# A transformer step on one core: the scale vector of the second norm made by VectorE in blocks of 256 features

## The chip, the core and the metric

The kernel runs on one core of a Trainium2 chip. The core has five engines with a queue of instructions each: TensorE (PE, matrix products; its weight loads are shown apart as PEld), VectorE (DVE), ScalarE (ACT), GpSimd (POOL) and SyncE (SP, which here only issues DMA transfers). An engine works its queue in order and waits for other engines and for transfers by semaphores. The metric is the device time of one execution in microseconds (us).

## What is computed

One layer of a hybrid backbone over 128 context and 512 latent tokens, with 2048 features, in float32. Each of the two halves of the layer is a norm with a scale and a shift, a mixer or a feed-forward net, and a norm with a gate:

```python
m = (jax.nn.silu(cv) @ w_ada + b_ada)[:, None, :]
sh1, sc1, g1, sh2, sc2, g2 = jnp.split(m, 6, axis=-1)     # one set for the context, one for the latents
h = rmsnorm(x, g_pre_mix) * (1 + sc1) + sh1
z = h @ w_in                                              # q, k, v of 8 heads; convolution; pooling
o = jnp.concatenate([a, cm, pm], axis=-1) @ w_out
x = x + g1 * rmsnorm(o, g_post_mix)
h = rmsnorm(x, g_pre_ffn) * (1 + sc2) + sh2
gt, up = jnp.split(h @ w_ffn_in, 2, axis=-1)
x = x + g2 * rmsnorm((jax.nn.silu(gt) * up) @ w_ffn_out, g_post_ffn)
```

The change is about `sc2`, the scale of the second norm: 2048 features for each of two conditionings, from a 2048 x 2048 slice of `w_ada` (16 MB).

## The kernel before

Features lie on the 128 partitions (16 tiles `kt`), tokens on the free axis, in two halves of 320. Each float32 product is made of three matmuls over high and low parts (`mm3`, L310 to L312): the weights of a *granule* (four tiles of 128 x 128) are split by ScalarE (L149, high) and VectorE (L150, low) into a tile `hl`. A list `items` is written in advance and worked off by `run_items`; before each item `prep_ahead` splits weights up to four granules ahead. Between granules `slot()` takes one step of each side task: convolution, pooling, `att_s` (scores, softmax, transposes to `pth`) and `att_v` (values, product `po`) of a head.

The order of the first part: pooling units and 24 units of q, k and v (`proj_unit`, four granules of 24 matmuls, loads of 512 KB on ScalarE's queue); then the output projection. Its first four feature blocks are worked in parts (`parts`, granules of 12 matmuls on the first half of the tokens), because the inputs come in late: `conv_final` (L493: a product on VectorE, then silu on ScalarE, then a split) makes the convolution's input and `put_cat` splits the stored outputs of heads and pooling. After two rounds of parts stands the pointwise product of the convolution (`wpw_use`, `cpw`), which needs the last split of `conv_final`. Then come plain granules for feature blocks 4 to 15 (first pass), and a second pass for the other half of the tokens, during which `chain` makes the second norm and first uses `sc2`.

The vectors of modulation 2, 3 and 4 (gate, shift, scale; `mods`) are made during the units: behind every second granule two items of 512 KB are loaded by SP into the ring `rb` of two buffers, and `mod1_use` (L204) multiplies each with the 32 columns of `s32` (two of them used) in four column tiles: four matmuls of 256 columns. After 32 items the sum lies in a bank, and `mod_finish` transposes it on VectorE and adds bias and gain. Vector 4, which is `sc2`, takes the last 32 items, in units 16 to 23 (heads 4 and 5, and q and k of head 6). Vector 5 is made later by VectorE (`mod5`, L1388 and L1390): blocks of 128 x 256, one instruction for each conditioning.

Of the kernel before, what the change touches and what calls it, by code (L numbers as in the profile page):

```python
# [16 lines left out]
P = 128  # L17
# [37 lines left out]
def trunk_kernel(ctx, tc, xT, small, wada0, wada1, wada2, win0, win, wout, wfi, wfo, ckT, cv, wpw, wpool, rpbT, invc,  # L55
# [283 lines left out]
    def proj_unit(src, evac, hooks):  # L339
        us = w_units(src)  # L340
        st = {}

        def use(g):
            def f(w):
                if g == 0:
                    st["ps"] = [bank("pj", "pj") for _ in range(2)]
                for hf in range(2):
                    for k in range(4):
                        kt = 4 * g + k
                        mm3(st["ps"][hf][:, :TH], w, k, act[hf][:, kt, 0, :], act[hf][:, kt, 1, :], kt == 0,  # L350
                            kt == KT - 1)
                if g == 3:
                    for hf in range(2):
                        evac(hf, st["ps"][hf])
                slot()
            return f
        for g in range(4):
            g_item(us[g // 2], g % 2, use(g))
            if g % 2:
                add_mods(2)  # L360
            if g in hooks:
                x_item(hooks[g])

    def x_item(f):
        items.append(("x", f))
# [5 lines left out]
    def opened(key, stack):  # L371
        P1[key] = stack.enter_context(tc.tile_pool(name=key, bufs=1, reuse_waits="tile"))
        return P1[key]
# [155 lines left out]
    def pool_side(g, up):  # L529
# [25 lines left out]
            act_e.activation(cat[:, s], ps[:, :TH], AF.Copy, scale=smv("pool_scale")[:, g:g + 1])  # L555
        act_e.dma_start(out=catd[g], in_=cat)

    def open_pool():
        accs.close()
        pm = opened("pm", pms)  # L560
        r = mxt([P, UP], "ps0", pool_=pm)[:, :4 * P].rearrange("p (g n) -> p g n", g=4)
        sp.dma_start(out=r, in_=wpool)
        t = cs["wpool"] = mxt([P, 2, 4, P], "wph", dt=F32R, pool_=pm)
        split(t[:, 0], t[:, 1], r)
# [198 lines left out]
        pool.dma_start(out=catd[4 + h if h < 4 else 8 + h], in_=cat)  # L763


    mods = [(v, kt, s) for v in (2, 3, 4) for kt in range(KT) for s in range(2)]

    def add_mods(n):

# [93 lines left out]
        P2["ss", 0] = p.tile([P, TH], F32, tag="ss", name="ss0")  # L863

    def begin_pass2():
        acts.close()
        q = XR.enter_context(tc.tile_pool(name="xr", bufs=1, side="right", reuse_waits="tile"))
        for i in (1, 2):
            t = q.tile([P, KP, 2, TH], F32R, tag=f"X{i}", name=f"X{i}")
            X[i] = [t[:, k] for k in range(KP)]  # L870
        add_slots(q, "r", KP)
        for k in range(KP):
            X["b", k] = slot_tile(f"ob{k}")
        P2["y2"] = yst.enter_context(tc.tile_pool(name="yp", bufs=1, side="right")).tile([P, TH], F32, tag="y2", name="y2")
        P3["e"] = eps.enter_context(tc.tile_pool(name="ep3", bufs=1, side="right", reuse_waits="tile"))
        p = P2["p", 1] = stb.enter_context(tc.tile_pool(name="ph2b", bufs=1, side="right", reuse_waits="tile"))
        P2["ss", 1] = p.tile([P, TH], F32, tag="ss", name="ss1")
        side.append(chain())
# [134 lines left out]
    def pass_unit(n, hf, parts=False):  # L1013
# [17 lines left out]
        us = w_units(wout[n])  # L1031
        for g in range(4):
            g_item(us[g // 2], g % 2, use(g))
            if hf and n == KT - 1 and g == 1:
                x_item(lambda: S3.fetch())

# [3 lines left out]
    for g in range(4):  # L1040
        if g == 2:
            us = w_units(wpw)
            for n in range(4):
                g_item(us[n // 2], n % 2, wpw_use(n))
        for i, p in enumerate(parts):
            p(g)
            if g < 2:
                x_item(lambda: next(fin, None))
            if g != 1:
                x_item(lambda: put_cat(1))  # L1050
# [947 lines left out]
```

## Time and profile before

| | |
|---|---|
| median of 3 runs | 2737.63 us (2736.96 to 2738.61) |
| the profiled execution | 2736.24 us, span of its trace 2734.5 us |
| TensorE busy | 2611.9 us (96%) |
| VectorE busy | 2027.8 us (74%) |
| ScalarE busy | 1192.6 us (44%) |
| column tiles of vectors 2 to 4 (L204) | 206.8 to 649.9 us, 768 records, 52.4 us busy |
| heads 4 to 7 | some 497 to 720 us |
| parts of the output projection | some 718 to 777 us |
| first plain pass | some 777 to 862 us |

Times in the trace are microseconds from the start of the span. A fp32 matmul has two records. "Idle before <- releaser" names what ended an engine's wait. A busy TensorE is not TensorE at its peak, since matmuls overlap; what a group of matmuls costs is read from the starts of the matmuls around it. The granted clock of TensorE is 1.00 for 2.4 GHz and 0.50 for 1.2 GHz.

### The profile page before, as it was taken

What the parts mean: (1) busy time and instruction counts of PE and PEld (TensorE: products, weight loads), DVE (VectorE), ACT (ScalarE), POOL (GpSimd) and SP (SyncE); (2) the same over time, 40 slices, a digit from 0 to 9 for tenths busy, and PEclk for the clock granted to TensorE, in tenths of its full rate; (3) what the DMA queues carried; (4) which work ended last, traced back from release to release, by engine and by line L of the source; (5) the groups of instructions that cost most, each with busy time, mean ns of one, the idle gap of its engine ahead of it and who ended that gap; (6) DMA issues with size and microseconds to landing.
All of it is one profiled execution on the core that took longest, in us unless ns stands there. A gap on an engine that the chain in (4) does not pass through costs nothing.

```text
span 2734.5 us, 48244 instructions
## 1 busy us (share of the span) xinstructions
PE 2611.9 (96%) x18874; PEld 2515.4 (92%) x18874; DVE 2027.8 (74%) x3248; ACT 1192.6 (44%) x2427; POOL 681.9 (25%) x572
## 2 busy tenths in 40 slices
PE   5999999999899988999999999999999899999996
PEld 4898998899899987999999999999999899999985
DVE  5558874443545779777888888888786899999966
ACT  4232333333554646333333333333333655555554
POOL 2300020000112435544333333333333111111112
PEclk9999999999999999999999999999999999999998
DMA  8856565653445774443333333333332433333343
GB/s 310 297 187 220 197 195 199 221 189 123 159 147 168 212 250 145 147 160 125 128 107 120 124 117 111 127 125 107 121 124 81 140 107 121 110 120 106 98 130 109
DMA packets 182708, 415.88 MB, mean 152 GB/s; under 512 B 17872, under 2 KB 99920, under 8 KB 181968
## 3 DMA queue, kind: packets, MB, share of 16 engines
q1 hardware_dynamic: 151568, 316.58, 35.2%
q10 hardware_dynamic: 27296, 82.33, 9.5%
q0 software_dynamic: 3616, 13.90, 1.4%
q8 instruction: 148, 2.42, 0.4%
q14 instruction: 80, 0.66, 0.1%
HBM read 373.01 MB, written 39.71 MB: 151 GB/s over the span
## 4 chain that ended last, share of the span: by engine, by line
PE 66%; DVE 17%; ACT 5%; issue 5%; DMA 3%; POOL 2%; ACTq 1%; SPq 0%; DVEq 0%; POOLq 0%
PE pj L310 7%; PE pj L311 7%; PE pj L312 7%; PE u L1167 7%; PE u L1165 7%; PE u L1166 7%; DVE hl L1122 5%; PE bb L1165 3%; PE bb L1167 3%; PE bb L1166 3%; ACT hl L1121 2%; DVE f L1390 2%; PE bc L1165 2%; PE bc L1167 2%; PE bc L1166 2%
## 5 line engine op out<-in xcount | busy, mean ns | idle before, releaser
L1167 PE MATMUL u<-X,hl 128*128 128x320 f32 x2464 | 767.6, 312 | 23.7 <-DVE hl L1122 23.4
L1165 PE MATMUL u<-X,hl 128*128 128x320 f32 x2464 | 767.6, 312 | 8.2 <-ACT hl L1121 4.5
L1166 PE MATMUL u<-X,hl 128*128 128x320 f32 x2464 | 762.8, 310 | 0.0
L310 PE MATMUL pj<-act,hl 128*128 128x320 f32 x1664 | 525.1, 316 | 8.8 <-ACT act L250 4.7
L311 PE MATMUL pj<-act,hl 128*128 128x320 f32 x1664 | 516.0, 310 | 1.2 <-DVE act L150 0.7
L312 PE MATMUL pj<-act,hl 128*128 128x320 f32 x1664 | 515.4, 310 | 0.0
L1167 PEld LDWEIGHTS u<-X,hl 128*128 128x128 f32 x2464 | 464.2, 188 | 34.7 <-DVE hl L1122 34.5
L1165 PEld LDWEIGHTS u<-X,hl 128*128 128x128 f32 x2464 | 464.2, 188 | 15.8 <-ACT hl L1121 8.1
L1166 PEld LDWEIGHTS u<-X,hl 128*128 128x128 f32 x2464 | 464.3, 188 | 0.3 <-issue 0.2
L310 PEld LDWEIGHTS pj<-act,hl 128*128 128x128 f32 x1664 | 314.1, 189 | 33.8 <-issue 15.7
L150 DVE TENSOR_TENSOR hl<-ra,hl 128x512 fp32r<-128x512 f32 x244 | 183.5, 766 | 191.8 <-ACT hl L149 191.3
L311 PEld LDWEIGHTS pj<-act,hl 128*128 128x128 f32 x1664 | 314.2, 189 | 3.5 <-DVE act L150 2.1
L312 PEld LDWEIGHTS pj<-act,hl 128*128 128x128 f32 x1664 | 314.2, 189 | 0.2 <-DVE hl L150 0.2
L1122 DVE TENSOR_TENSOR hl<-ra,hl 128x512 fp32r<-128x512 f32 x264 | 244.0, 933 | 43.0 <-ACT hl L1121 42.5
L1150 POOL TENSOR_TENSOR s<-ra 128x512 f32<-128x512 f32 x88 | 145.0, 1647 | 335.0 <-DMA ra<-in_wfi 116.9
L1121 ACT ACTIVATE hl<-ra 128x512 fp32r<-128x512 f32 x264 | 159.4, 625 | 132.0 <-PE u L1167 106.0
L1121 ACT ACTIVATE hl<-s 128x512 fp32r<-128x512 f32 x176 | 110.2, 626 | 236.7 <-DVE s L1147 197.3
L1122 DVE TENSOR_TENSOR hl<-s,hl 128x512 fp32r<-128x512 f32 x176 | 133.4, 762 | 82.0 <-ACT hl L1121 80.9
L149 ACT ACTIVATE hl<-ra 128x512 fp32r<-128x512 f32 x244 | 148.2, 631 | 100.8 <-PE pj L312 56.9
L1122 DVE TENSOR_TENSOR hl<-sy,hl 128x512 fp32r<-128x512 f32 x176 | 139.2, 791 | 67.6 <-ACT hl L1121 67.2
L1147 POOL TENSOR_TENSOR sy<-ra,sy 128x512 f32<-128x512 f32 x88 | 133.7, 1519 | 151.4 <-DVE hl L1122 151.4
L1150 POOL TENSOR_TENSOR T<-T,raw 128x384 f32<-128x384 f32 (+1 forms) x56 | 54.8, 979 | 457.2 <-DVE T L1150 438.0
(343 smaller groups left out, 4926.3 us busy)
## 6 DMA issues: line engine op xcount, KB each, us to landing
ra<-in_wfi SPq DMA_DIRECT2D x196, 512.0 KB, 4.2
rb<-in_wada SPq DMA_DIRECT2D x96, 512.0 KB, 5.5
ra<-in_wada SPq DMA_DIRECT2D x64, 512.0 KB, 6.2
ra<-in_win ACTq DMA_DIRECT2D x56, 512.0 KB, 4.8
ra<-in_wout ACTq DMA_DIRECT2D x56, 512.0 KB, 4.1
raw<-in_wfo SPq DMA_DIRECT2D x48, 576.0 KB, 4.0
f<-in_wada SPq DMA_DIRECT2D x128, 128.0 KB, 2.1
fd<-f ACTq DMA_DIRECT2D x44, 320.0 KB, 2.2
```

The lines of the kernel that those rows point to most:

```text
L149: act_e.activation(h, src, AF.Copy)
L150: dve.tensor_tensor(out=l, in0=src, in1=h.bitcast(F32), op=ALU.subtract)
L310: pe.matmul(ps, w[:, 0, k, :], rhs_h, start=start, stop=False)
L311: pe.matmul(ps, w[:, 0, k, :], rhs_l, start=False, stop=False)
L312: pe.matmul(ps, w[:, 1, k, :], rhs_h, start=False, stop=stop)
L1121: act_e.activation(g.hl[:, 0, :n], src, AF.Copy)
L1122: dve.tensor_tensor(out=g.hl[:, 1, :n], in0=src, in1=g.hl[:, 0, :n].bitcast(F32), op=ALU.subtract)
L1147: e.tensor_tensor(out=out, in0=a, in1=b, op=ALU.subtract)
L1150: e.tensor_tensor(out=out, in0=a, in1=b, op=ALU.add)
L1165: pe.matmul(ps, w[:, 0, j, :], xh, start=first and j == 0, stop=False, skip_group_check=True)
L1166: pe.matmul(ps, w[:, 0, j, :], xl, start=False, stop=False, skip_group_check=True)
L1167: pe.matmul(ps, w[:, 1, j, :], xh, start=False, stop=stop and j == n - 1, skip_group_check=True)
```

## The change

Vector 4 leaves `mods`. In units 16 to 27 one or two steps (`dm_step`) stand behind each granule (1, 2, 1, 2), behind each part and behind each plain granule of the first pass one. A step takes one block of 128 x 256 weights from a ring of two buffers `dw` and runs two VectorE instructions, one for each conditioning: the first time for a column range it writes `macc`, later it multiplies with a scalar of `s32` and adds. Then SP loads the block after next into the buffer that this step has read. The two accumulators take the place of the ring `rb`. After 64 steps (half of the features), `dm_finish` sums over the partitions by eight matmuls with 32 columns of ones, and VectorE transposes and adds bias and gain. 128 steps make the vector: 72 in units 16 to 27, 16 in the parts, 40 in the plain pass.

```diff
             g_item(us[g // 2], g % 2, use(g))
-            if g % 2:
+            if not mods:
+                dm_item(1 + g % 2)
+            elif g % 2:
                 add_mods(2)
...
+    def dm_fetch(n):
+        for s, kt, j in DMS[dm["f"]:dm["f"] + n]:
+            t = dm["p"].tile([P, 256], F32, tag="dw", bufs=2, name="dw")
+            sp.dma_start(out=t, in_=wada1[2, kt, s][:, 256 * j:256 * j + 256])
+            dm["raw"].append(t)
+            dm["f"] += 1
+
+    def dm_step(n):
+        for s, kt, j in DMS[dm["c"]:dm["c"] + n]:
+            if kt == 0 and j == 0:
+                dm["acc"] = [wpb.tile([P, 1024], F32, tag="rb", bufs=2, name="macc") for _ in range(2)]
+                if s == 0:
+                    dm_fetch(2)
+            raw = dm["raw"].pop(0)
+            for c in range(2):
+                a, w = dm["acc"][c][:, 256 * j:256 * j + 256], s32[:, kt, c:c + 1]
+                if kt == 0:
+                    dve.tensor_scalar(out=a, in0=raw, scalar1=w, scalar2=None, op0=ALU.mult)
+                else:
+                    dve.scalar_tensor_tensor(out=a, in0=raw, scalar=w, in1=a, op0=ALU.mult, op1=ALU.add)
+            dm["c"] += 1
+            dm_fetch(1)
+            if kt == KT - 1 and j == 3:
+                dm_finish(s)
+
+    def dm_finish(s):
+        ps = bank("md", "mod4")
+        for c in range(2):
+            for j in range(4):
+                pe.matmul(ps[32 * j:32 * j + 32, 256 * c:256 * c + 256], ones[:, :32], dm["acc"][c][:, 256 * j:256 * j + 256],
+                          start=c == 0, stop=c == 1, tile_position=(0, 32 * j), skip_group_check=True)
...
+    def dm_item(n):
+        if n:
+            x_item(lambda: dm_step(n))
...
-    mods = [(v, kt, s) for v in (2, 3, 4) for kt in range(KT) for s in range(2)]
+    mods = [(v, kt, s) for v in (2, 3) for kt in range(KT) for s in range(2)]
...
             g_item(us[g // 2], g % 2, use(g))
+            if not hf:
+                dm_item(1)
...
         for i, p in enumerate(parts):
             p(g)
+            dm_item(1)
```

TensorE's queue in a unit of heads 4 to 6, before: `mod` is the bank of the vector, `rb` the weights, `s_90` the conditioning, `pj` the bank of the unit, `act_80` and `act_81` the two halves of the tokens.

```order
L310 MATMUL pj<-act_81,hl 128x320
L311 MATMUL pj<-act_81,hl 128x320
L312 MATMUL pj<-act_81,hl 128x320
L204 MATMUL mod_4_5520<-rb,s_90 32x256 x8
L310 MATMUL pj<-act_80,hl 128x320
L311 MATMUL pj<-act_80,hl 128x320
```

Sixteen such groups of eight go; on TensorE there are now two, at the ends of the two halves, here in head 7:

```order
L310 MATMUL pj<-act_81,hl 128x320
L311 MATMUL pj<-act_81,hl 128x320
L312 MATMUL pj<-act_81,hl 128x320
L594 MATMUL mod_7546<-macc,ones 32x256 x8
L310 MATMUL pj<-act_80,hl 128x320
L311 MATMUL pj<-act_80,hl 128x320
```

The groups of 32 columns that stood behind every second granule now stand twice in all, and read `macc` in place of loaded weights.

VectorE's queue in the parts of the output projection, before (`hl<-ra` is the split of a granule's weights, `cac` holds the convolution's reciprocal deviation, `qhl` and `khl` two of its four inputs):

```order
L150 TENSOR_TENSOR hl<-ra,hl 128x512
L493 TENSOR_TENSOR qhl<-qhl,cac 128x640
L150 TENSOR_TENSOR hl<-ra,hl 128x512
L150 TENSOR_TENSOR act_80<-qhl,act_80 128x320
L150 TENSOR_TENSOR act_81<-qhl,act_81 128x320
L150 TENSOR_TENSOR hl<-ra,hl 128x512
L493 TENSOR_TENSOR khl<-khl,cac 128x640
```

The same place after the change:

```order
L150 TENSOR_TENSOR hl<-ra,hl 128x512
L584 SCALAR_TENSOR_TENSOR macc<-dw,s_90,macc 128x256 x2
L495 TENSOR_TENSOR qhl<-qhl,cac 128x640
L150 TENSOR_TENSOR hl<-ra,hl 128x512
L584 SCALAR_TENSOR_TENSOR macc<-dw,s_90,macc 128x256 x2
L150 TENSOR_TENSOR act_80<-qhl,act_80 128x320
L150 TENSOR_TENSOR act_81<-qhl,act_81 128x320
L150 TENSOR_TENSOR hl<-ra,hl 128x512
L584 SCALAR_TENSOR_TENSOR macc<-dw,s_90,macc 128x256 x2
L495 TENSOR_TENSOR khl<-khl,cac 128x640
```

A step of two instructions now stands behind each split of weights, ahead of the product of `conv_final` (now L495) and of the `act` splits.

SP's queue from head 7 to the output projection, after the change (before, the four loads from `cvd` followed the load of `cvt` directly, and no loads of `dw` stood behind them):

```order
L669 DMA out_nkT<-kC 128x128
L568 DMA dw<-in_wada 128x256 x6
L651 DMA out_nvT<-vF 128x128
L785 DMA cvt<-in_cv 128x128
L568 DMA dw<-in_wada 128x256 x2
L492 DMA chp<-cvd 128x640
L492 DMA qhl<-cvd 128x640
L492 DMA khl<-cvd 128x640 x2
L568 DMA dw<-in_wada 128x256 x54
```

The loads for `conv_final` moved behind two loads of blocks, each of which waits for a step on VectorE.

## Rows read from the trace of the kernel before

**Rows 1.** Busy time by stage: the stretch, its length, then busy us (instructions) of TensorE, its weight loads, VectorE, ScalarE and GpSimd, the granted clock of TensorE, the DMA share and GB/s. The stretches are the end of head 6, head 7 with the seam, the parts, and the first plain pass.

```profile
655.00:700.00 45.00, 45.00 (x309) 44.57 (x308) 16.70 (x40) 16.38 (x57) 4.61 (x8) 1.00 0.18 54
700.00:730.00 30.00, 24.17 (x156) 22.23 (x154) 20.70 (x53) 19.94 (x57) 5.91 (x11) 0.95 0.71 234
730.00:770.00 40.00, 38.18 (x243) 36.77 (x241) 21.73 (x43) 24.29 (x56) 1.08 (x2) 0.95 0.43 127
800.00:860.00 60.00, 60.00 (x411) 60.00 (x410) 25.39 (x35) 27.69 (x60) 7.94 (x9) 1.00 0.51 151
```

**Rows 2.** Instructions of TensorE in order of time from 720 to 772 us, those ahead of which it stood idle (in brackets: us and what ended it).

```profile
720.24 0.33 PE L712 MATMUL ptr<-ident,pt 128*128 128x128 f32 x1 [0.22 <-DVE pt L651]
...
729.69 0.69 PE L712 MATMUL ptr<-ident,pt 128*128 128x128 f32 x2 [4.86 <-DVE pth L715]
...
748.04 0.41 PE L310 MATMUL cpw<-act,hl 128*128 128x320 f32 x1 [1.43 <-ACT act L149]
...
771.13 0.42 PE L310 MATMUL pj<-act,hl 128*128 128x320 f32 x1 [0.49 <-ACT act L149]
```

**Rows 3.** TensorE around one group of column tiles in order of time, a weight load of another group that waited for its transfer, and the group of all such matmuls from 503 to 652 us (count, busy us, mean ns).

```profile
533.75 0.31 PE L312 MATMUL pj<-act,hl 128*128 128x320 f32 x1
533.99 1.07 PE L204 MATMUL mod<-rb,s 128*32 128x256 f32 x16
534.99 0.41 PE L310 MATMUL pj<-act,hl 128*128 128x320 f32 x1
535.25 0.31 PE L311 MATMUL pj<-act,hl 128*128 128x320 f32 x1
535.39 0.31 PE L312 MATMUL pj<-act,hl 128*128 128x320 f32 x1
...
526.19 0.16 PEld L204 LDWEIGHTS mod<-rb,s 128*32 128x32 f32 x8 [0.98 <-DMA rb<-in_wada]
...
L204 PE MATMUL mod<-rb,s 128*32 128x256 f32 x256 | 17.5, 386 | 0.5 <-DMA rb<-in_wada 0.5
```

**Rows 4.** The instructions by which VectorE makes vector 5 (ns least, median, most; first and last start), two of them and the next one in order of time, SP's load of the block after next behind them and the loads of 512 KB that follow it, and the time to landing of all such loads of 128 KB.

```profile
L1390 DVE SCALAR_TENSOR_TENSOR f<-f,vec,f x240: 469/476/1529, 1292.0 to 2049.0; 128x256 f32<-128x256 f32 x120
...
L1388 DVE TENSOR_SCALAR f<-f,vec x16: 340/344/1453, 1284.9 to 1966.0; 128x256 f32<-128x256 f32 x16
...
1307.49 0.87 DVE L1390 SCALAR_TENSOR_TENSOR f<-f,vec,f 128x256 f32<-128x256 f32 x2
1308.29 0.68 DVE L1122 TENSOR_TENSOR hl<-ra,hl 128x512 fp32r<-128x512 f32 x1
...
1308.39 0.33 SPq L1376 DMA_DIRECT2D f<-in_wada  x1
1308.83 0.85 SPq L1093 DMA_DIRECT2D ra<-in_wfi  x2
...
DMA to landing us min/median/max: 1.9/2.1/5.0
```

**Rows 5.** Head 6, in order of time: VectorE's last split before the scores and its first instruction on them, the last division of the softmax, and TensorE's transposes that need it.

```profile
652.19 0.68 DVE L150 TENSOR_TENSOR hl<-ra,hl 128x512 fp32r<-128x512 f32 x1
654.29 0.29 DVE L645 TENSOR_REDUCE rs<-scc 128x1 f32<-128x128 f32 x1 [0.27 <-PE scc L677]
667.55 0.42 DVE L651 TENSOR_SCALAR pt<-pt,rs 128x384 f32<-128x384 f32 x1
...
670.62 0.82 PE L712 MATMUL ptr<-ident,pt 128*128 128x128 f32 x6
```

**Rows 6.** VectorE in head 7 in order of time: the instructions ahead of which it stood idle for something other than ScalarE's half of a split of weights.

```profile
704.08 0.29 DVE L645 TENSOR_REDUCE rs<-scc 128x1 f32<-128x128 f32 x1 [0.20 <-PE scc L677]
...
704.71 0.56 DVE L641 CUSTOM_DVE_ANT_0 pt<-sc,mb 128x384 f32<-128x384 f32 x1 [0.15 <-PE sc L684]
...
708.93 0.69 DVE L641 CUSTOM_DVE_ANT_0 pt<-sc,mb 128x512 f32<-128x512 f32 x1 [0.55 <-PE sc L684]
...
715.23 0.56 DVE L641 CUSTOM_DVE_ANT_0 pt<-sc,mb 128x384 f32<-128x384 f32 x1 [0.32 <-issue]
...
724.98 0.29 DVE L150 TENSOR_TENSOR vhl<-cvt,vhl 128x128 fp32r<-128x128 f32 x1 [0.54 <-ACT vhl L149]
```

**Rows 7.** VectorE in the parts, in order of time, over one loop of two parts.

```profile
736.65 0.82 DVE L493 TENSOR_TENSOR qhl<-qhl,cac 128x640 f32<-128x640 f32 x1
738.97 0.69 DVE L150 TENSOR_TENSOR hl<-ra,hl 128x512 fp32r<-128x512 f32 x1 [1.51 <-ACT hl L149]
739.58 0.89 DVE L150 TENSOR_TENSOR act<-qhl,act 128x320 fp32r<-128x320 f32 x2
740.39 0.68 DVE L150 TENSOR_TENSOR hl<-ra,hl 128x512 fp32r<-128x512 f32 x1
740.99 0.82 DVE L493 TENSOR_TENSOR khl<-khl,cac 128x640 f32<-128x640 f32 x1
```

**Rows 8.** The stretch behind TensorE's gap of 4.86 us (columns as in rows 1), and the fifteen `po` matmuls on the chain that ended last (start, us), in head 6 and in head 7.

```profile
731.00:733.00 2.00, 2.00 (x9) 1.81 (x8) 1.80 (x5) 1.27 (x4) 0.00 (x0) 0.50 0.63 167
...
683.56 2.45 PE po L753 x15
...
730.63 3.88 PE po L753 x15
```

**Rows 9.** VectorE in the last parts, in order of time.

```profile
767.10 0.69 DVE L150 TENSOR_TENSOR hl<-ra,hl 128x512 fp32r<-128x512 f32 x1 [0.33 <-ACT hl L149]
767.71 0.89 DVE L150 TENSOR_TENSOR act<-kF,act 128x320 fp32r<-128x320 f32 x2
768.93 0.69 DVE L150 TENSOR_TENSOR hl<-ra,hl 128x512 fp32r<-128x512 f32 x1 [0.33 <-ACT hl L149]
```

**Rows 10.** Time to landing of the loads of 160 KB (`xt`) in the second pass, least, median and most.

```profile
DMA to landing us min/median/max: 3.0/3.4/4.9
```

More of the change, by code (lines that the diff above doesn't have):

```diff
@@ L556, in pool_side @@
         act_e.dma_start(out=catd[g], in_=cat)
+    dms = ExitStack()
+    dm = {"raw": [], "f": 0, "c": 0}
+    DMS = [(s, kt, j) for s in range(2) for kt in range(KT) for j in range(4)]
+    def dm_fetch(n):
[27 more added lines that the diff above has]
+                          start=c == 0, stop=c == 1, tile_position=(0, 32 * j), skip_group_check=True)
+        t, h = mtmp["f"](), KT // 2
+        dve.transpose(t[:, :512], ps)
+        tv = t[:, :512].rearrange("p (c b r) -> p c b r", c=2, r=32)
+        for c in range(2):
+            d = modT[:, 4, h * s:h * s + h, c]
+            dve.tensor_tensor(out=d, in0=tv[:, c, :, 0], in1=smv("b_ada")[:, 4 * KT + h * s:4 * KT + h * s + h], op=ALU.add)
+            dve.scalar_tensor_tensor(out=d, in0=d, scalar=1.0, in1=smv("g_pre_ffn")[:, h * s:h * s + h], op0=ALU.add,
+                                     op1=ALU.mult)
+    def dm_item(n):
+        if n:
+            x_item(lambda: dm_step(n))
     def open_pool():
         accs.close()
+        dm["p"] = dms.enter_context(tc.tile_pool(name="dm", bufs=1, side="right", reuse_waits="tile"))
         pm = opened("pm", pms)
@@ L865, in begin_pass2 @@
     def begin_pass2():
+        assert dm["c"] == len(DMS)
+        dms.close()
         acts.close()
```

## The prediction

> **What bounds the kernel now.** I read the share of each engine by stage first, then the order in time at the places that the change touches. In the heads and in the first pass of the output projection TensorE is the bound: from 655 to 700 us it is busy 45.00 of 45 us, from 800 to 860 us 60.00 of 60, while VectorE stands at 16.70 and 25.39 us [rows 1]. The reader is to see that the stretch of 655 to 700 us holds no column tiles any more and is still full: taking TensorE work out of 505 to 650 us uncovers no other limit by itself. Between the heads and the plain passes it is otherwise. From 700 to 770 us TensorE is busy 24.17 of 30 and 38.18 of 40 us [rows 1], and its gaps end with VectorE or ScalarE: 4.86 us for `pth`, 1.43 us for `act` [rows 2]. There the work goes back and forth between VectorE and ScalarE, and that stretch lies on the path that sets the end. The change takes time from the bound engine in a full stretch and adds work to VectorE in three: the later heads, this seam, and the first plain pass.
>
> **What is removed.** Sixteen groups of eight column-tile matmuls (16 records each; 256 records in all from 503 to 652 us [rows 3]). One group costs this: without it a matmul starts 0.146 us after the one before; with it L312 starts at 533.75, the next L310 at 534.99 and L311 at 535.25 [rows 3]. That is (1.24 - 0.146) + (0.26 - 0.146) = 1.21 us, and sixteen are 19.4 us. One group was also held up by its weights (0.98 us between its halves [rows 3], some 0.6 us of it beyond the usual distance); with a smaller second case I put 0.8 us for these waits. Gain: **20.2 us**. That the matmuls are gone is seen in the order of instructions, so this part needs no faith.
>
> **What is added on TensorE.** Two closing groups of eight matmuls in the same 32-column form, one in the last head, one in the first plain pass: 2 x 1.21 = 2.4 us. At both places VectorE stands ahead of TensorE in the trace of before (its splits are made four granules ahead), so I add no wait for the last sum. A wait of one step, 0.87 us each [rows 4], is the upper bound.
>
> **What is added on VectorE.** 128 steps of two instructions on 128x256 blocks: 240 scalar_tensor_tensor and 16 tensor_scalar. The kernel already runs the former in this shape for another vector: 476 ns, two together 0.87 us, and the next instruction starts 0.80 us after the first [rows 4]. The latter takes 344 ns [rows 4], overlapped the same way 0.53 us a pair. All steps come to about 100 us: 72 steps in heads 4 to 7, 16 in the parts of the output projection, 40 in its first plain pass.
>
> *Heads 4 to 6.* The softmax chain has slack in the trace of head 6, which has no column tiles beside it: the last division ends at 667.97, the transposes start at 670.62 [rows 5], 2.65 us. Steps of 1.60, 0.80, 1.60 and 0.80 us lie in the chain ahead of that point, 4.8 us, of which waits for scores (0.15, 0.55, 0.53 us as in head 7 [rows 6]) and the free time before the scores (652.8 to 654.2 in head 6 [rows 5]) take about 2.6. So some 2.2 us of 2.65 are used: no stall in heads 5 and 6. Head 4 has the convolution's last sums beside it, and SP's queue holds loads that wait for a store, behind which a block's load stands. I take 1.5 us in all; the bounds are 0 and 6 (two such waits in each of three heads).
>
> *Head 7 and the seam to 736 us.* Here TensorE already waits for divisions and for `pth` [rows 2], so a delay is paid in full. In order: two steps of 0.53 less waits of 0.35, then 0.53 less 0.55, then 0.53 + 0.80 less 0.32, then 0.80: 2.5 us late at the divisions [rows 6]. Then 1.60 (two steps) and one of 0.80 less 0.54 ahead of the next `pth`, and 0.80 ahead of the last: **5.2 us**.
>
> *The parts from 736 to 749 us.* Each pair of parts is one loop: split, L493, ScalarE's silu and split, split, two `act` splits, split, and L493 again; L493 starts at 736.65 and at 740.99 [rows 7], 4.34 us. A step stands behind each split, and no idle time of VectorE lies where it could go: the wait of 1.51 us [rows 7] is ScalarE's work that itself waits for L493. Six steps until TensorE's gap at 748.04 [rows 2]: **4.8 us**. That gap then grows from 1.4 to over 6 us. The gap of 4.86 us was followed by a granted clock of 0.50 (the 1.2 GHz level) [rows 8], under which fifteen `po` matmuls took 3.88 us on the chain where they take 2.45 [rows 8]. I add one more such fall, **1.5 us**, as the matmuls behind the gap are TensorE-bound.
>
> *The parts from 764 to 772 us.* A loop of 1.83 us (splits at 767.10 and 768.93) with 0.33 us idle [rows 9]. Four steps, three of which fill that idle time: 3 x 0.47 + 0.80 = **2.2 us**.
>
> *First plain pass.* A granule is 12 matmuls, 12 x 0.146 = 1.75 us; VectorE then has 0.61 + 0.80 us in it, so it keeps up if the data does. A block's buffer is free again after the step (0.87), SP's issue (0.03, from 1308.36 to 1308.39), the landing and some 0.05 us; with two buffers a landing of up to 3.50 - 0.95 = 2.55 us costs nothing. For the same size and row length the trace has 1.9 at least, 2.1 as the median and 5.0 at most [rows 4]; 160 KB in the next pass takes 3.4 [rows 10]. I take the median, as it is the same transfer, and **1.0 us** for a few late ones. The Trainium skill, "DMA: Bandwidth & Descriptors" (section "Anatomy of one DMA"), gives a transfer 2.0 us plus its bytes at 436 GB/s, a fit made for GpSimd's path; by that estimate 128 KB lands in 2.3 us, below the 2.55, and by it this term is 0 and the sum 1.0 us better; the 2.1 us of the trace agree.
>
> The 32 loads of 512 KB that go and the 128 of 128 KB that come are the same bytes. SP loses waits for TensorE and gets waits for VectorE; behind them stand the loads of `kF`, `cvt` and the four of `conv_final`, which now go out after the last steps of head 7 (some 5 us later; they are needed about as much later).
>
> **Sum.** 20.2 - 2.4 - 1.5 - 5.2 - 4.8 - 1.5 - 2.2 - 1.0 = 1.6 us gained. The profiled execution took 2736.24 us (span 2734.5); it becomes 2734.6. The median of the runs is 1.39 us higher, so I forecast **2736.0 us**: no difference that can be told, since about 0.2% (5.5 us) is what a measurement of this kernel separates from no change.
>
> **Rivals.** *A, the seam hides the steps.* VectorE idles 9.3 and 18.3 us of 700 to 770 us [rows 1], more than the steps there need. If they slide into idle time that I counted as bound, half of 5.2 + 4.8 + 2.2 and the fall of the clock go: 1.6 + 6.1 + 1.5 = 9.2 us gained, 2728.4; with all of it hidden 2722. For it: my chain adds delays one after the other; against it: the order puts each step ahead of the instruction that ScalarE or TensorE waits for.
> *B, the round trip of a block.* With only two buffers VectorE waits for data in the first plain pass. At the 3.4 us of the 160 KB loads [rows 10] a step comes every (0.95 + 3.4) / 2 = 2.18 us instead of 1.75; forty cost 17.0, less 3.5 us of lead (two granules): 13.5 instead of 1.0, so 2748.5. It decides from a landing of 2.55 us. For it: 512 KB loads of `wout` run beside it all the time; against it: the 2.1 us were taken beside such loads too. The Trainium skill's page named above (section "Bandwidth") says to batch transfers to 1 MiB and so speaks against blocks of a quarter of the size; it would do what rival B does.
> *C, the heads' chain.* If the steps make TensorE wait in heads 4 to 7 by the bound of 6 us and by a block's load behind SP's waits some 4 us more, it is 8.5 us worse: 2744.5.
> *D, nothing moves*: the matmuls' place is filled by waits of the same length; the order of instructions gives no sign.
>
> **How the numbers follow.** Forecast 0.39 (its own range 2732 to 2742), A 0.32, B 0.15, C 0.12, D 0.02. Faster 0.32 (A), same 0.41 (forecast and D), slower 0.27 (B and C). The range of 2725 to 2748 holds the forecast, most of A, C and half of B.
>
> **What would show it.** Right: about 18 us less TensorE time up to 650 us; no new gaps there; the gap before the `cpw` matmul over 6 us, with a second fall of the granted clock; first plain pass at 1.75 us a granule. Wrong: gaps in the heads that end with VectorE (C); VectorE waiting for `dw` in the plain pass, landing above 2.55 us (B); a seam no longer than before (A).

## The result and the profile after

| | us |
|---|---|
| before, median of 4 runs beside it | 2738.12 (2736.96 to 2742.0) |
| after, median of 4 runs | 2771.52 (2767.86 to 2774.57) |
| ratio after to before | 1.0122, 95% interval 1.0108 to 1.0135 |
| profiled execution after | 2767.86, span 2766.0 |

The change costs 33 us, far outside the range of 2725 to 2748. To see where, I split the trace at four matmuls that both kernels have: the first of the pooling product (`plo`, still ahead of the change; 231.44 us before, 229.67 after), the scores `scc` of head 7 (703.66, 694.93), the last `cpw` (761.37, 765.22) and `oss`, which follows the first pass (864.34, 896.09). The lengths between them changed so: **heads** -7.0 us, **seam** +12.6, **plain pass** +27.9. The third length holds the last eight parts of the output projection too: split again at the 97th matmul behind the last `cpw`, where the plain granules begin, it is +6.5 for these parts and +21.4 for the plain granules. This split is used for all runs below, from one execution of each; over the heads it has a spread of some 2 us (the control at the end, which changes nothing there, shows -2.4). late_ring6, ra_pool and before_ra had one disturbed execution each (3639 us and more), which their medians leave out, and late_ring6, whose trace was taken in it, has no split.

The windows of the profile after, columns as in [rows 1]:

```profile
655.00:700.00 45.00, 44.70 (x310) 42.77 (x309) 30.50 (x73) 17.83 (x62) 7.49 (x12) 1.00 0.39 112
700.00:730.00 30.00, 19.30 (x106) 16.78 (x105) 23.30 (x60) 17.06 (x47) 3.74 (x7) 0.84 0.74 250
730.00:770.00 40.00, 33.77 (x210) 32.53 (x210) 21.91 (x45) 19.71 (x44) 1.08 (x2) 0.91 0.34 98
...
800.00:860.00 60.00, 53.86 (x353) 51.52 (x351) 44.95 (x86) 22.45 (x49) 6.58 (x7) 1.00 0.62 184
```

The last row is the largest change: from 800 to 860 us TensorE starts 353 matmuls, where it started 411 [rows 1]. Twelve, one granule, now take 60 / 353 x 12 = 2.04 us and not 1.75. VectorE's busy time rose from 25.39 to 44.95 of 60 us, so by its share VectorE is not full either. What the two wait for, in the view of waits from 777 to 882 us (us in total, times, longest):

```profile
DVE macc L584 <- DMA dw<-in_wada: 20.0, 20, 2.0
...
PEld pj L312 <- DVE hl L150: 8.4, 8, 1.5
...
PE pj L312 <- DVE hl L150: 6.3, 7, 1.2
PE mod L594 <- DVE macc L584: 6.3, 4, 3.2
```

VectorE waits 20 times for a block; TensorE in turn waits for the low half of the weights (`hl`), so the four granules by which VectorE was ahead are used up. In order of time on VectorE:

```profile
808.97 0.87 DVE L584 SCALAR_TENSOR_TENSOR macc<-dw,s,macc 128x256 f32<-128x256 f32 x2
809.76 0.68 DVE L150 TENSOR_TENSOR hl<-ra,hl 128x512 fp32r<-128x512 f32 x1
811.08 0.88 DVE L584 SCALAR_TENSOR_TENSOR macc<-dw,s,macc 128x256 f32<-128x256 f32 x2 [0.63 <-DMA dw<-in_wada]
811.88 0.68 DVE L150 TENSOR_TENSOR hl<-ra,hl 128x512 fp32r<-128x512 f32 x1
812.48 0.88 DVE L584 SCALAR_TENSOR_TENSOR macc<-dw,s,macc 128x256 f32<-128x256 f32 x2
813.27 0.68 DVE L150 TENSOR_TENSOR hl<-ra,hl 128x512 fp32r<-128x512 f32 x1
815.05 0.88 DVE L584 SCALAR_TENSOR_TENSOR macc<-dw,s,macc 128x256 f32<-128x256 f32 x2 [1.09 <-DMA dw<-in_wada]
```

Every second step waits. The time to landing of these blocks from 777 to 880 us (least, median, most):

```profile
DMA to landing us min/median/max: 2.0/2.5/5.0
```

At the end of the pass stands the second closing sum. TensorE, in order of time:

```profile
870.55 1.06 PE L594 MATMUL mod<-macc,ones 128*32 128x256 f32 x2 [3.16 <-DVE macc L584]
872.03 1.06 PE L594 MATMUL mod<-macc,ones 128*32 128x256 f32 x2 [0.42 <-DVE macc L584]
874.83 1.06 PE L594 MATMUL mod<-macc,ones 128*32 128x256 f32 x2 [1.74 <-DVE macc L584]
```

TensorE reaches it before VectorE's last steps and waits between its pieces. In the window of these 10 us the granted clock fell to 0.53, close to the level of 1.2 GHz, and 21 matmuls started where 70 fit:

```profile
870.00:880.00 10.00, 6.35 (x21) 2.42 (x22) 6.98 (x15) 3.19 (x7) 0.96 (x1) 0.53 0.65 193
```

In the heads the gain of the matmuls is lost late. At the scores `scc` of heads 4 to 7, counted from `plo`, the change stands 7.1, 11.0, 10.9 and 7.0 us ahead of the kernel before; the run no_steps below, which has no steps at all, stands 5.8, 13.0, 20.4 and 20.4 us ahead. So 7.5 us are lost from the scores of head 5 to those of head 6, and this is the place, in head 5: SP's queue, ScalarE and TensorE in order of time.

```profile
577.81 5.79 SPq L568 DMA_DIRECT2D dw<-in_wada  x4
583.64 0.43 SPq L666 DMA_DIRECT2D kF<-in_ckT  x1
```

```profile
587.97 0.84 ACT L149 ACTIVATE khl<-kF 128x768 fp32r<-128x768 f32 x1 [3.39 <-DMA kF<-in_ckT]
```

```profile
588.86 0.69 PE L736 MATMUL sc<-khl,qhl 128*128 128x384 f32 x1 [4.55 <-ACT khl L149]
...
590.66 0.47 PE L310 MATMUL pj<-act,hl 128*128 128x320 f32 x1
590.92 0.47 PE L311 MATMUL pj<-act,hl 128*128 128x320 f32 x1
```

SP holds four loads of blocks, each behind a step of VectorE, then loads `kF`; ScalarE waits 3.39 us for it, TensorE 4.55 us for ScalarE, and after that the matmuls start 0.26 us apart and not 0.146 (granted clock 0.50 from 588 to 592 us). From 590 to 600 us 54 matmuls start where 70 fit, which is some 2.3 us more. In the seam TensorE's gaps are those of [rows 2], longer:

```profile
712.41 0.41 PE L310 MATMUL pj<-act,hl 128*128 128x320 f32 x1 [3.21 <-ACT act L149]
...
727.31 0.69 PE L764 MATMUL ptr<-ident,pt 128*128 128x128 f32 x2 [6.38 <-DVE pth L767]
...
745.02 0.41 PE L311 MATMUL cpw<-act,hl 128*128 128x320 f32 x1 [1.14 <-DVE act L150]
750.63 0.63 PE L310 MATMUL cpw<-act,hl 128*128 128x320 f32 x1 [5.05 <-ACT act L149]
```

### The profile page after: what moved, and what is told of

The parts are those of the page before. It is cut to its first block, busy times and chain, and to the rows that moved or that the text cites. A ratio compares the mean times of both kernels' runs of the same rounds, so it can differ in the third digit from the quotient of the medians.

```text
span 2766.0 us, 48288 instructions
## 1 busy us (share of the span) xinstructions
PE 2614.0 (95%) x18650; PEld 2519.1 (91%) x18650; DVE 2139.2 (77%) x3509; ACT 1192.3 (43%) x2427; POOL 681.0 (25%) x572
## 4 chain that ended last, share of the span: by engine, by line
PE 58%; DVE 20%; DMA 7%; issue 6%; ACT 6%; POOL 2%; ACTq 0%; SPq 0%; DVEq 0%; POOLq 0%
PE u L1224 6%; PE u L1222 6%; PE u L1223 6%; PE pj L310 5%; DVE hl L1179 5%; PE pj L311 5%; PE pj L312 5%; DMA dw<-in_wada 3%; PE bb L1222 3%; PE bb L1224 3%; PE bb L1223 3%; ACT hl L1178 2%; DVE f L1447 2%; PE bc L1222 2%; PE bc L1224 2%
## 5 line engine op out<-in xcount | busy, mean ns | idle before, releaser
L310 PE MATMUL pj<-act,hl 128*128 128x320 f32 x1664 | 526.5, 316 | 12.8 <-ACT act L149 4.6
L310 PEld LDWEIGHTS pj<-act,hl 128*128 128x128 f32 x1664 | 315.7, 190 | 33.5 <-issue 12.8
L150 DVE TENSOR_TENSOR hl<-ra,hl 128x512 fp32r<-128x512 f32 x244 | 182.6, 754 | 133.8 <-ACT hl L149 133.0
L1179 DVE TENSOR_TENSOR hl<-ra,hl 128x512 fp32r<-128x512 f32 x264 | 252.7, 967 | 37.8 <-ACT hl L1178 37.2
```

What stands on the lines that cost most here:

```text
L150: dve.tensor_tensor(out=l, in0=src, in1=h.bitcast(F32), op=ALU.subtract)
L310: pe.matmul(ps, w[:, 0, k, :], rhs_h, start=start, stop=False)
L1179: dve.tensor_tensor(out=g.hl[:, 1, :n], in0=src, in1=g.hl[:, 0, :n].bitcast(F32), op=ALU.subtract)
```

## The experiments

The theory after the result: the ring of two buffers (rival B) makes VectorE wait for blocks in the plain pass, and SP's order (rival C) does so in the heads. Its rival: the data is no matter, VectorE's added instructions are. All times are medians; the lengths are changes against the kernel before, in the order heads, seam, plain pass.

| run | us | ratio to before (95%) | heads, seam, plain pass |
|---|---|---|---|
| the change | 2771.52 | 1.0108 to 1.0135 | -7.0, +12.6, +27.9 |
| no_steps | 2725.55 | 0.9940 to 0.9970 | -20.4, +5.0, +2.0 |
| no_reload | 2746.91 | 1.0022 to 1.0048 | -18.4, +10.3, +17.6 |
| ring6 | 2763.41 | 1.0078 to 1.0108 | -5.6, +12.9, +20.0 |
| pool_queue | 2779.33 | 1.0136 to 1.0169 | -10.7, +13.3, +41.6 |
| late_close | 2763.92 | 1.0080 to 1.0113 | -6.7, +12.8, +19.9 |
| late_ring6 | 2756.09 | 1.0047 to 1.0087 | no split |
| ra_pool | 2735.71 | 0.9981 to 1.0001 | -17.6, +11.9, +7.3 |
| lead6 | 2794.23 | 1.0188 to 1.0223 | +11.8, +16.3, +30.6 |
| lead6_late | 2749.89 | 1.0026 to 1.0056 | -13.6, +12.7, +10.1 |
| lead4_late | 2746.50 | 1.0015 to 1.0040 | -15.5, +12.2, +10.0 |
| lead4_late_ra | 2741.89 | 0.9998 to 1.0016 | -14.5, +13.1, +4.1 |
| late_ring6_ra | 2746.68 | 1.0016 to 1.0040 | -6.4, +12.8, +3.4 |
| ra_only | 2768.47 | 1.0107 to 1.0135 | -5.2, +14.2, +24.2 |
| before_ra | 2735.51 | 0.9985 to 1.0004 | -2.4, +0.5, -1.7 |
| seam_free | 2740.49 | 1.0008 to 1.0026 | -1.6, 0.0, +3.0 |
| parts_free | 2735.72 | 0.9987 to 1.0005 | -7.8, +3.1, +3.0 |
| spread | 2733.13 | 0.9969 to 0.9988 | -10.9, +3.1, +2.5 |

**What the removal is worth: no_steps.** No loads of blocks, no VectorE steps and no closing matmuls: `dm_step` only counts, and `dm_finish` fills the vector from bias and gain.

```diff
-            raw = dm["raw"].pop(0)
-            for c in range(2):
...
             dm["c"] += 1
-            dm_fetch(1)
```

> Leaves out the steps, their loads and the closing sums altogether (the vector is made from bias and gain alone): what the removal of the column tiles is worth by itself. My sum put it at 20.2 us: 2718 us. If other work takes the place of the matmuls in the heads (only 5 us of the some 18 due by then were seen there), it stays above 2730 us.

The heads gain 20.4 us, the 20.2 of the sum. But the whole gains 12.4: 5.0 us go in the seam and 2.0 in the last parts without any step; the plain granules lose nothing. In the windows from 700 us TensorE, there earlier, still waits (its longest wait is 4.8 us for `pth`, as before), and three slices of 10 us stand at a granted clock of 0.83, where before only those from 720 to 740 us lay below 1.00 (0.84 and 0.82):

```profile
700.00:710.00 10.00, 6.83 (x34) 5.80 (x34) 7.51 (x18) 7.38 (x23) 2.14 (x4) 0.83 0.91 303
710.00:720.00 10.00, 7.81 (x42) 7.34 (x43) 5.95 (x12) 6.22 (x20) 0.54 (x1) 0.83 0.41 153
...
730.00:740.00 10.00, 8.32 (x44) 8.10 (x45) 3.09 (x6) 4.15 (x10) 0.00 (x0) 0.83 0.10 30
```

**Data or instructions: no_reload, ring6, pool_queue.** In the first, all steps read two blocks that are loaded once:

```diff
-            raw = dm["raw"].pop(0)
+            raw = dm["raw"][dm["c"] % 2]
...
-            dm_fetch(1)
```

> Leaves out all loads of blocks but the first two: every step reads one of these two, so the 128 steps with their 256 VectorE instructions and both closing sums stay, and no step waits for a transfer (the vector is made from two blocks of weights only). Theory B with C (the round trip of a block, and SP's loads behind waits for steps): the plain pass gives back most of its 28 us and the heads most of their 12 us, so 2732 to 2742 us. Rival (VectorE's 100 us of added work, in its queue ahead of the splits, is what costs): within 5 us of the changed kernel, 2765 to 2773 us.

In the second the ring grows when the heads' buffers are gone:

```diff
+        dm["p"] = dms.enter_context(tc.tile_pool(name="dm2", bufs=1, side="right", reuse_waits="tile"))
+        dm["n"] = 6
+        dm_fetch(4)
```

> From the end of the parts on, the blocks go through a ring of six buffers and not two; heads and parts are left as they are, and the whole vector is made. Theory B (round trip of two buffers in the plain pass): 20 to 28 us of the 28 lost there come back, 2744 to 2752 us, and VectorE no longer waits for blocks there. Rival (VectorE's added work, or ScalarE's and VectorE's splits waiting for each other): the plain pass stays within 5 us of the changed kernel, 2766 to 2772 us.

In the third GpSimd issues the loads:

```diff
-            sp.dma_start(out=t, in_=wada1[2, kt, s][:, 256 * j:256 * j + 256])
+            pool.dma_start(out=t, in_=wada1[2, kt, s][:, 256 * j:256 * j + 256])
```

> The loads of blocks are issued by GpSimd and not by SP, so the loads of kF, cvt and the convolution's inputs no longer stand behind waits for steps. Theory C: the heads gain 4 to 10 us (ScalarE's split of the scores' keys no longer waits for a load of kF), 2761 to 2768 us; the plain pass stays as slow, since the ring still has two buffers. Rival (SP's order costs nothing in the heads): within 3 us of the changed kernel, or slower by GpSimd's own work that now stands behind the waits.

Neither theory holds alone. Without waits for blocks 24.6 us come back, nearly all of the heads' loss, but the plain pass stays 17.6 us longer (13.4 of it in the plain granules); six buffers give back 8 us there, not 20 to 28. That the heads gain by the waits and not by the 16 MB that are not moved, lead4_late shows below: it loads every block, and its heads stand 15.5 us ahead. So in the plain pass something else binds nearly as hard. The trace of no_reload shows it, ScalarE and VectorE in order of time (ACTq is ScalarE's queue of DMA issues):

```profile
803.91 0.33 ACTq L130 DMA_DIRECT2D ra<-in_wout  x1
804.35 1.15 ACT L149 ACTIVATE hl<-ra 128x512 fp32r<-128x512 f32 x2 [2.39 <-DVE macc L584]
807.13 0.33 ACTq L130 DMA_DIRECT2D ra<-in_wout  x1
...
811.52 0.33 ACTq L130 DMA_DIRECT2D ra<-in_wout  x1
811.95 1.16 ACT L149 ACTIVATE hl<-ra 128x512 fp32r<-128x512 f32 x2 [2.39 <-DVE macc L584]
```

```profile
803.20 0.68 DVE L150 TENSOR_TENSOR hl<-ra,hl 128x512 fp32r<-128x512 f32 x1
803.80 0.87 DVE L584 SCALAR_TENSOR_TENSOR macc<-dw,s,macc 128x256 f32<-128x256 f32 x2
805.01 0.69 DVE L150 TENSOR_TENSOR hl<-ra,hl 128x512 fp32r<-128x512 f32 x1 [0.34 <-ACT hl L149]
805.62 0.88 DVE L584 SCALAR_TENSOR_TENSOR macc<-dw,s,macc 128x256 f32<-128x256 f32 x2
806.41 0.69 DVE L150 TENSOR_TENSOR hl<-ra,hl 128x512 fp32r<-128x512 f32 x1
```

The low half on VectorE ends at 803.88 and frees a buffer of `ra`; only then ScalarE issues the load of `wout` that stands ahead of its next high halves (804.35), and only after that VectorE has work for its next low half (805.01). It is one loop of two engines. A load brings the weights of two granules, so there are two low halves in each round, and the step between them (805.62) lengthens it: the low half behind this step ends at 807.10, and the next load goes out at 807.13. The step behind the second low half (803.80) costs nothing, since VectorE still waits 0.34 us behind it. ScalarE's high halves come 7.60 us apart for four granules (804.35 to 811.95), 1.90 us each, above TensorE's 1.75. By an estimate from these rows the loop without its two steps of 0.80 us takes 7.60 - 1.60 = 6.0 us, 1.50 a granule, and does not bind. (The wait is put down to `macc`; what had to come first is the split. In ra_pool below, where GpSimd issues these loads, its waits ahead of them are put down to `hl`, 13 times from 790 to 850 us.)

pool_queue loses in the plain pass: a block's time to landing is 3.5 us there in place of 2.5 (777 to 880 us), so the round trip of two buffers grows. That this is what costs the 13.7 us is argued, not shown: from 777 to 882 us VectorE's waits for blocks are as long in all as in the change (19.5 and 20.0 us), those for ScalarE's halves are longer (16.2 and 6.9 us). In the heads it gains 3.7 us, a little less than the 4 to 10 expected; from the scores of head 5 to those of head 6 it gets back 5.4 of the 7.5.

```profile
L568 POOL DMA_DIRECT2D dw<-in_wada x40: 536/538/556, 778.7 to 877.8; - x40
...
DMA to landing us min/median/max: 2.4/3.5/4.7
```

**The closing sum and the loop: late_close, late_ring6, ra_pool, ra_only, before_ra.** The second sum moves behind the first unit of the second pass (late_close; late_ring6 with six buffers too):

```diff
-            if kt == KT - 1 and j == 3:
+            if kt == KT - 1 and j == 3 and s == 0:
...
+        if n == 0:
+            x_item(lambda: dm_finish(1))
```

> Only the second closing sum moves: from the end of the first plain pass to behind the first unit of the second pass, where VectorE's last step is some 30 us old. Theory (this sum stands on TensorE right behind a step that is not yet done, and the clock falls behind that wait): the stretch at the end of the plain pass with few matmuls goes, 6 to 9 us gained, 2762 to 2766 us. Rival (VectorE is late there anyway, and TensorE waits as long for the splits that follow): within 2.5 us of the changed kernel, 2769 to 2774 us.

> Both: six buffers from the end of the parts on, and the second closing sum behind the first unit of the second pass. Six buffers alone gave 2763.4 us. If the late sum is worth 6 to 9 us of its own, 2754 to 2758 us; if the two take the same loss away, 2761 to 2764 us.

The sum's place costs 7.6 us of its own, and six buffers another 7.8. The loads of `wout` in the first plain pass go to GpSimd, on top of no_reload (ra_pool), of the change (ra_only) and of the kernel before (before_ra):

```diff
-        us = w_units(wout[n])
+        us = w_units(wout[n], None if hf else pool)
```

> As the run without reloads (two blocks for all steps, 2746.9 us, no wait for blocks), and in the first plain pass the loads of wout are issued by GpSimd and not by ScalarE. Theory (ScalarE and VectorE run one loop there: ScalarE's next split stands behind a load whose buffer VectorE's split frees, VectorE's split waits for ScalarE's, and the steps lengthen this loop to 1.90 us a granule, above TensorE's 1.75): the loop opens, VectorE gets ahead again, TensorE is full to the end of the pass, 8 to 15 us gained, 2732 to 2739 us. Rival (VectorE's own instructions are the bound): within 3 us of 2746.9 us.

> The changed kernel with one edit: the loads of wout in the first plain pass are issued by GpSimd. Two buffers and the closing sum at the end of the pass stay. If the loop of ScalarE and VectorE comes first in the plain pass (at the median landing of 2.5 us two buffers just suffice for 1.75 us a granule): 8 to 14 us gained, 2757 to 2764 us. If the round trip of the two buffers comes first: within 4 us of the changed kernel, 2767 to 2774 us.

> A control: the kernel before, with the loads of wout in the first plain pass issued by GpSimd. TensorE is full there already (60.00 of 60 us), so nothing is to be gained: 2735 to 2741 us. If the other queue is worth something by itself, below 2733 us, and the same sum comes off the gains that I read from it in the other runs.

With no wait for blocks the open loop gives 11.2 us. On the change as it is it gives nothing that can be told: VectorE still waits for blocks there (770 to 900 us):

```profile
DVE macc L584 <- DMA dw<-in_wada: 22.5, 22, 2.3
```

So of the two cases in ra_only that of the round trip holds: the two limits lie one behind the other, the blocks first. The control shows that the queue by itself is worth nothing.

**Blocks early, sums late, in the heads: lead6, lead6_late, lead4_late.** The accumulators of one strip of 256 features take half a tile of the old ring, two strips one tile; the other tile gives four more buffers. Eight closing sums of two matmuls each.

```diff
-    DMS = [(s, kt, j) for s in range(2) for kt in range(KT) for j in range(4)]
+    DMS = [(s, j, kt) for s in range(2) for j in range(4) for kt in range(KT)]
...
+            i = dm["f"] % 6
+            t = dm["p"].tile([P, 256], F32, tag="dw", bufs=2, name="dw") if i < 2 else dm["big"][:, 256 * (i - 2):256 * (i - 1)]
...
+            if kt == KT - 1:
+                dm_finish(s, j)
```

> Six buffers from the first step on: the blocks go strip by strip (256 features after another), so two strips of accumulators take one tile of the old ring and four more buffers the other; eight closing sums of two matmuls each in place of two of eight. Theory (the heads lose their 10 us or so by VectorE waiting for blocks): by the scores of head 7 the kernel is 17 to 20 us ahead of the kernel before where the changed one is 9 ahead, and with the plain pass as with six buffers the whole takes 2751 to 2757 us. Rival (the heads lose by SP's order, kF's loads behind waits for steps): head 7 stays at 9 to 12 us ahead, and the whole at 2760 to 2766 us.

Both expectations missed: slower by 23 us than the change, though VectorE hardly waits for blocks. TensorE comes to most closing sums before VectorE is done: seven of the eight wait, 4.7 to 7.2 us each. In order of time, and as a wait from 480 to 720 us:

```profile
609.31 1.92 PE L596 MATMUL mod<-macc,ones 128*32 128x256 f32 x4 [5.45 <-DVE macc L584]
```

```profile
PE mod L596 <- DVE macc L584: 17.4, 3, 7.1
```

Then each sum eight steps later (the last behind the first unit of the second pass), with six blocks on the way or four:

```diff
-            if kt == KT - 1:
-                dm_finish(s, j)
+            if dm["c"] % 16 == 8 and dm["c"] > 16:
+                k = dm["c"] // 16 - 1
+                dm_finish(k // 4, k % 4)
...
-                dm_fetch(6)
+                dm_fetch(4)
```

> Strips with six buffers again, but each closing sum stands eight steps behind the last step of its strip (the last one behind the first unit of the second pass). Theory (that run lost by its eight closing sums, each of which TensorE reached before VectorE had done the steps; 17.4 us of such waits from 480 to 720 us): these waits go, the heads stand 17 to 20 us ahead of the kernel before at the scores of head 7, and the whole takes 2743 to 2750 us. Rival (the strips lose by something else, such as four more buffers that make SP load more at once beside the projections' weights): above 2770 us.

> As that, with four blocks on the way and not six, so that SP's load waits for a step two earlier and seldom holds kF's loads up. Theory of SP's order in the heads: 3 to 6 us faster than with six on the way. Theory of the round trip alone: the same within 2 us, since no step waits for a block in either.

The place of the sums alone was worth 44.3 us (2794.23 to 2749.89). Four on the way gain 3.4 us more by the medians, but the intervals overlap (1.0026 to 1.0056 and 1.0015 to 1.0040), so what SP's order is worth between these two is not shown. ScalarE's waits for `kF` (480 to 720 us) point the same way: 7.2 us in the change, 2.1 in lead6_late, 0.7 in lead4_late.

**All together: lead4_late_ra, late_ring6_ra.** lead4_late, and the change with six buffers and the late sum, each with the loads of `wout` by GpSimd.

> As that, with the loads of wout in the first plain pass issued by GpSimd and not by ScalarE. All four suspected costs (round trip, SP's order, late closing sums, the loop of ScalarE and VectorE) are taken away, and the steps' own instructions stay: 2730 to 2737 us, at or below the kernel before; what stays above 2725.6 us (no steps at all) is the seam's. If the losses found so far aren't the whole, above 2742 us.

> The changed kernel's order of blocks and two buffers in the heads, with six buffers from the end of the parts on, the late second closing sum, and the loads of wout by GpSimd. Without the last it was 2756.9 us. Theory of the loop: 5 to 11 us less, 2746 to 2752 us (the loop also held TensorE behind VectorE when no block was waited for). Rival (six buffers and the late sum have taken all of that away): 2755 to 2758 us.

The plain pass is back to +4.1 and +3.4 us, the plain granules to +2.5 and 0.0; the second run is 9.4 us faster than late_ring6, so with the blocks in time the loop is the next limit in the real kernel too. lead4_late_ra is no slower than the kernel before, but misses its 2730 to 2737 us: the seam keeps +13.1.

**Where the steps stand: seam_free, parts_free, spread.** lead4_late_ra with the steps given out by a list (steps behind each granule of units 16 to 27), none in the parts, and one behind each plain granule (spread: two behind one of four in eight units):

```diff
-                dm_item(1 + g % 2)
+                dm_item(plan.pop(0))
...
-            dm_item(1)
...
+    plan = [2, 2, 2, 3] * 9 + [0] * 12
```

> As the run with all four costs taken away (2741.9 us), with no step from the units of head 7 to the end of the parts: 81 steps in heads 4 to 6 (2, 2, 2 and 3 a unit), 47 in the plain pass. Theory (the steps in the seam cost 7 to 8 us there, as 13 us are lost in the seam with them and 5 without any): 2732 to 2736 us, faster than the kernel before. Rival (heads 4 to 6 at 9 steps a unit pay as much as the seam got back): 2739 to 2744 us.

> As that, with 72 steps in heads 4 to 6 (2 behind each granule), 9 in head 7 and 47 in the plain pass; none in the parts. If the price in the seam is the parts' (each step there stands ahead of an instruction that ScalarE waits for), within 2 us of the run without steps in the seam. If head 7 has its share, some 3 us above it.

> As the run with no steps in the parts (2735.7 us), with 63 steps in heads 4 to 6 (1, 2, 2, 2 a unit), 9 in head 7 and 56 in the plain pass. If the heads' price falls with each step a unit (8 a unit kept 9 us of the 20 at the scores of head 7, 6 a unit kept 15), some 3 us come back in the heads, and VectorE's 1.5 us a granule in the plain pass still fit beside TensorE's 1.75: 2731 to 2735 us, just faster than the kernel before. Rival (what the heads give the plain pass takes): 2735 to 2740 us.

`plan` is as shown in seam_free, `[2] * 36 + [0, 1, 1, 1] * 3` in parts_free, `[1, 2, 2, 2] * 9 + [0, 1, 1, 1] * 3` in spread. parts_free came out 4.8 us faster than seam_free, which neither of its two cases had. Without steps the seam costs nothing, but at 9 steps a unit the heads lose nearly all of the 20 us, so that TensorE comes to the seam no earlier than before. At 8 a unit the heads keep 7.8 us, at 7 a unit 10.9, at the 6 of lead4_late_ra 14.5. spread is faster than the kernel before, by 0.1 to 0.3%; it is the best version found. Its windows, columns as above:

```profile
655.00:700.00 45.00, 45.00 (x311) 44.71 (x310) 24.81 (x57) 17.77 (x63) 6.71 (x12) 1.00 0.37 118
...
730.00:770.00 40.00, 38.17 (x257) 37.41 (x256) 22.92 (x41) 27.79 (x63) 6.78 (x11) 1.00 0.42 128
800.00:860.00 60.00, 59.02 (x393) 56.96 (x392) 52.27 (x106) 25.85 (x55) 12.02 (x17) 1.00 0.72 222
```

VectorE is busy 52.27 of 60 us in the plain pass and TensorE nevertheless 59.02, with 393 matmuls started where the change had 353 and the kernel before 411: busy VectorE was not the main trouble there, waiting VectorE was.

## Why the prediction was wrong

**What is removed, 20.2 us: right as a size, wrong as a gain.** 20.4 us by the scores of head 7 (no_steps), but 12.4 at the end. The sentence that taking work out "uncovers no other limit by itself" looked only at 655 to 700 us. The seam behind it takes 5.0 us back and the last parts 2.0; what there sets these waits was not taken apart.

**Closing groups, "I add no wait for the last sum": wrong.** I read that VectorE stands four granules ahead. The splits are four granules ahead, the last step before a sum is not: lead6 shows waits of up to 7.1 us in the heads, where VectorE is not full. (My reading, argued from the order alone: a step stands behind a split that needs a buffer which TensorE frees late.) Here the second sum's wait is not one step of 0.87 us but 6.3 us and a fall of the clock behind it; moving it gives 7.6 us.

**Heads 4 to 6, 1.5 us (0 to 6): wrong.** Of the 20.4 us only 7.0 are left, so 13.4 are lost up to head 7's scores, where 1.5 and 1.2 for the first closing sum were due. The steps' own instructions are the small part, 2.0 us (no_reload). The rest, 11.4 us, goes when the loads go (no_reload): waits of VectorE for blocks, and loads of `kF` behind waits for steps, as the rows of head 5 show. I had named that queue and priced it at next to nothing in the sum; rival C had the mechanism, its 10 us about the size. The larger part lies at that one place: 7.5 us are lost from the scores of head 5 to those of head 6, and the waits of 4.55 and 0.31 us there with the 2.3 us of the slow stretch behind them make 7.2; with SP's order changed (pool_queue) 5.4 of them come back. How the rest divides between the two is open. And the slack I read in head 6 [rows 5] does not reach further than the 6 steps a unit of the change: with sums late and blocks early the heads lose 5.9 us of the 20.4 at 6, 12.6 at 8 and 18.8 at 9 (these hold the strips' closing sums). One term of that reading was wrong, without weight: the third wait for scores is 0.32 us in [rows 6], not 0.53.

**Seam, 5.2 + 4.8 + 1.5 = 11.5 us up to the last `cpw`: the size was near (12.6), in part by luck.** The sum had nothing for what the seam takes from a kernel that comes to it earlier: no_steps loses 5.0 us there without any step, coming 20.4 us early; seam_free, without steps there and 1.6 us early, loses 0.0. How much of the 5.0 belongs to the change, which comes 7.0 us early, no run shows. The gap ahead of `cpw` grew from 1.43 to 1.14 + 5.05 us, "over 6" as foretold, with a fall of the clock behind it (0.78 from 750 to 760 us). Without the parts' steps and with half of head 7's the seam is at +3.1 (parts_free, 7.8 us early).

**Last parts, 2.2 us: too small, 6.5 measured.** 2.0 of these come without any step. With the loads of `wout` by GpSimd the last parts are 3.6 to 4.7 us shorter in three pairs of traces (no_reload 4.3 and ra_pool 0.7, lead4_late 5.3 and lead4_late_ra 1.6, the change 6.5 and ra_only 1.8), so loads on ScalarE's queue cost there too.

**First plain pass, 1.0 us: the step that failed most, 21.4 measured with the second sum's 1.2, nothing of it without any step.** Two sentences carry it. "I take the median": at two buffers a landing above 2.55 us is paid, and here 21 of the 43 landings from 777 to 880 us were above it (median 2.5, longest 5.0), so VectorE waited 20 times. The trace of before could have warned: behind the median of 2.1 in [rows 4] 35 of 126 landings are above 2.55. The Trainium skill, "DMA: Bandwidth & Descriptors" (section "Anatomy of one DMA"), gives 2.3 us by an estimate; the trace's median lies above it, and the spread, which no single figure has, did the harm. "VectorE then has 0.61 + 0.80 us in it, so it keeps up if the data does": it does not, since ScalarE's load waits for VectorE's low half, every second step stands in the loop that this closes, and the loop takes 1.90 us a granule. Rival B had the mechanism of the first, with a step every 2.18 us; a granule took 2.04, but the loop has its share in that, so the nearness is partly luck. Its 2748.5 missed the loop and the sum. Taken away in this order, the three causes come back nearly one by one: late sum 7.6, six buffers 7.8, GpSimd's queue 9.4 us (a part of the last in the last parts).

By stretches: the heads were to stand 20.2 - 1.5 - 1.2 = 17.5 us ahead and stand 7.0 (10.5 worse), the seam up to the last `cpw` was to cost 11.5 and costs 12.6 (1.1 worse), the last parts 2.2 and cost 6.5 (4.3 worse), the plain granules with the second sum 2.2 and cost 21.4 (19.2 worse): 35.1 us, which is the 1.6 forecast as gained and the 33.5 lost.

The Trainium skill, "Trainium Kernel Development and Optimization" (section "Key Constraints"), says that issuing transfers from several engines only saves the issuing time. before_ra agrees (0.9985 to 1.0004); late_ring6_ra does not, with 9.4 us: what the other queue saved was a split's wait behind the issue.

## What to carry to other kernels

When work is added to an engine that has time to spare, don't compare its busy time with the bound engine's: write down the loop that it closes with other engines, the issues of transfers in their queues among them, and see whether the added step lies in it. Count a ring's round trip with the late landings, not the median, and put a sum over partitions well behind the last instruction that it reads. Work taken out of a full stretch is worth only what the next unfilled stretch lets through.

## What was not expected of the hardware

One wait of a few us ahead of a small group of matmuls was followed by a stretch at the level of 1.2 GHz. In the profile after the granted clock was 0.53 from 870 to 880 us: it had come to 0.50 by 871 us, behind the first wait of 3.16 us, and stayed there through the shorter ones. In no_reload it was 0.50 from 850 to 860 us, behind a first wait of 2.38 us. And the same load of 128 KB landed 1.0 us later by the median when GpSimd issued it (3.5 for 2.5 us), its issue taking 0.54 us and not SP's 0.33. The landing is not fixed for SP either: with six buffers on the way it took 3.6 us by the median from 777 to 880 us (ring6), and VectorE waited for none of them in the plain granules.
